# A hybrid attention layer: two query tiles of each band-attention head turned by VectorE and DMA instead of TensorE, and attention's outputs stored in one piece

## The chip, the cores and the metric

The kernel runs on one core of one Trainium2 chip. The metric is device time in microseconds (us) of one execution; less is better. Three runs of the kernel before gave 814.21, 815.94 and 815.33 us, with a median of 815.33.

The engines are TensorE (PE; its weight loads are shown as PEld), VectorE (DVE), ScalarE (ACT), GpSimd (POOL) and SyncE (SP), which issues all the DMAs of this kernel.

## What is computed

One layer on a prompt of 1024 frames and on a sample of 32 frames (with 512 cached keys and values), all in float32. Cut to what matters here:

```
[qA kA vA gA qB kB vB gB] = rmsnorm(h) @ w_in        # 1024 x 4096
A, 8 heads of 64: s = q k^T / 8 + bias[clip(k_pos - q_pos)]
                  a frame reads its own 64-frame chunk and the 8 chunks before it
                  w = softmax(s);  oA = w v
B, 8 heads of 64: z = q k^T / 8, strictly causal
                  w = sigmoid(z) * prod over later keys of sigmoid(-z);  oB = w v
y = concat(oA * silu(gA), oB * silu(gB)) @ w_out
h = h + rmsnorm(y)
h = h + sigmoid(h @ w_ple_gate) * (p @ w_ple)
```

The outputs are h of prompt and sample, and the new keys and values.

## The kernel before

**Numbers.** A float32 product is made of float32r products: each operand is split into a rounded part and a rest ("h" and "l" in the names), and two or three products are added in PSUM.

**Stages.** After a start that normalises x and turns it, the projection w_in is computed in columns of 128 outputs (`col_steps`, L715): one column is three chunks of 352 frames, each of 24 matmuls into a PSUM bank "mm" (two banks). Two heads of A or B are a pair; the eight pairs come in the order A0, B0, A1, B1, A2, B2, A3, B3 (L1160). While a pair's attention runs, the three columns k, q, v of the next pair are woven in (`weave`, L1228), and in the last stage the eight gate columns. Pairs with an odd number also carry the sample's attention for four heads (`sample_attention`, L926); the first four stages carry sums of w_out and w_ple_gate on POOL (`sum_weights`, L1264). At the end come the output projection and the gate, by a seven-product scheme.

**One head's attention** (`attention`, L781) has eight query tiles of 128. For A, tile i reads the key blocks max(0, i - 4) to i (`lo_block`), so tiles 4 to 7 have five blocks each. `scores(i)` (L798) makes the scores in PSUM banks "S", adds bias and takes the maximum on DVE into w0 (name "om"), takes the exponential on ACT into w1 ("be") and scales w1 on POOL. `weights_t(i)` (L845) turns w1, block by block: up to four PE transposes into a PSUM bank "T" (ptw), then ACT copies the rounded part to wTh and DVE takes the rest to wTl. `values(g)` (L882) multiplies four query tiles at once into the bank "PV" (PVA, PVB), and the result goes out in two halves of 256 columns: an ACT copy, a DVE add (the products of rounded and rest parts of v lie in different partitions) and a store to `o_dr`. Tiles are turned two units after their scores (LAG_T) and a group of four gets its values right behind its last tile's turn (LAG_V).

**Room.** w0 and w1 come from rings (`Arena`, L212) of 3076 and 3384 columns of 128 partitions, handed out in order from the front and again from the front when the end is reached; a new tile waits for the last use of all that it covers. wTh and wTl are rings of 33 blocks. The sample's cached keys and values lie in w1's ring, too. A head of A needs 30 blocks of 128 columns in each ring.

**Order.** Nothing is run in program order. A recorder (L268) takes down all operations, and `order` (L375) is a list planner: each engine has an estimated cost for each operation (`cost`, L342), PE takes attention (class 0) before columns (class 1) and then the lower program index, the other engines the lower index, and each takes the best of what is ready. A DMA holds SP for ISSUE ns, and its data count as there after DMA_NS, its size over DMA_RATE and DMA_MARGIN. The order found is fixed in the program: each engine runs its list strictly in that order, and an instruction that waits holds all behind it on its engine. All instructions are recorded at L453, so views by line show one line, and names tell them apart (the pair's number and the head are left out of the names: SA, ptwA, otB).

**Another place that turns by squares.** `values_out` (L681) turns v, 128 x 1024: DVE transposes 32 x 32 squares (vx), a store to a scratch in DRAM (swap), four loads that put the squares' rows in place, one for each quarter of the partitions, and an ACT copy that also restores the order of the blocks. `weights_t` holds the same path for a tile, behind `swapped`, which is always False.

Of the kernel before, what the change touches and what calls it, by code (L numbers as in the profile page):

```python
# [28 lines left out]

def swapped(ab, p, h, i):  # L30

    return False

LAG_T = 2
# [148 lines left out]
MARGIN = 400  # L185
ISSUE = 450
DMA_NS, DMA_RATE, DMA_MARGIN = 1500, 320.0, 2000
# [271 lines left out]
def stream_step(  # L459
# [321 lines left out]
    def attention(ab, p, h):  # L781
# [13 lines left out]
        def lo_block(i):  # L795
            return max(0, i - 4) if ab == "A" else 0

        def scores(i):  # L798
            L, kd, kl = Lq[h], KDh[h], KLD[h]
# [45 lines left out]
        def weights_t(i):  # L845
            g = i // 4
            step, size = LAID[ab, g]
            if g not in wT:
                wT[g] = [x.tile([P, size * P], f"{x.name}{nm}_{g}") for x in (ringh, ringl)]
            b0 = lo_block(i)  # L850
            w0, w1 = state.pop(i)
            n = i + 1 - b0
            at_ = ((i - 4 * g) * step + b0) * P
            hi, lo = (x[:, at_:at_ + n * P] for x in wT[g])
            if swapped(ab, p, h, i):

                nc.vector.transpose(w0[:, 0:n * P].rearrange("p (c b q) -> p b c q", c=4, q=32), w1)
                dr = scratch([P, n * P], f"swap{nm}_{i}")
                dma(dr, w0[:, 0:n * P])
                for c in range(4):  # L860
                    x = dr[:, c * n * 32:(c + 1) * n * 32].rearrange("(g k) x -> k g x", k=32)
                    dma(w1[32 * c:32 * c + 32].rearrange("k (g x) -> k g x", g=4), x)
                src = w1.rearrange("p (g b q) -> p g b q", g=4, q=32)
                hi, lo = (x.rearrange("p (b g q) -> p g b q", g=4, q=32) for x in (hi, lo))
                nc.scalar.copy(hi, src)
                nc.vector.tensor_tensor(lo, src, f(hi), ALU.subtract)
# [15 lines left out]
        def values(g):  # L882
# [20 lines left out]
        def cost(i):  # L903
            return i + 1 - lo_block(i)

# [20 lines left out]
    def sample_attention(ab, gi):  # L926
# [45 lines left out]
        def scores():  # L972
# [31 lines left out]
            dma(Vc, cv[0, 0, :, h4, :].rearrange("(b p) h d -> p b (h d)", p=P))  # L1004
            vn = at.tile([NS, 256], F32, tag="ot", name="vn" + nm, bufs=3)
            dma(vn, vs_dr[ab][:, 256 * gi:256 * gi + 256])
# [33 lines left out]
        def values():  # L1040
            acc = psum("PV", f"PV{nm}")[:, 0:256]
            for b, (w, v) in enumerate(bx["wv"]):
                for x, y in ((0, 0), (0, 1), (1, 0)):
                    nc.tensor.matmul(acc, w[x], v[y], start=(b + x + y == 0), stop=(b == 4 and x == 1))
            for h in range(4):
                src = acc[h * NS:(h + 1) * NS, h * HD:(h + 1) * HD]
                (nc.scalar.copy if h % 2 else nc.vector.tensor_copy)(diag[0:NS, h * HD:(h + 1) * HD], src)

        def out():
            pt = psum("T", f"pto{nm}")  # L1050
            for a in range(2):
                nc.tensor.transpose(pt[:, a * P:(a + 1) * P], diag[:, a * P:(a + 1) * P], ident)
            Os = at.tile([P, 2, NS], F32, tag="ot", name="O" + nm, bufs=3)
            nc.vector.tensor_copy(Os, pt[:, 0:2 * P].rearrange("p (a q) -> p a q", a=2)[:, :, 0:NS])
# [249 lines left out]

    ones = at.tile([P, P], F32R, tag="ot", name="ones", bufs=3)
    nc.gpsimd.memset(f(ones), 1.0)
# [520 lines left out]
```

## Time and profile before

| | |
|---|---|
| median of 3 runs | 815.33 us (814.21 to 815.94) |
| profiled execution | 815.1 us, its span 813.3 us |
| mean granted TensorE clock | 0.998 |
| DMA | 135.83 MB, 55.7% of 16 engines' span |
| DMAs issued by SP | 620 |

A row of a group of instructions reads: line, engine, operation, tile written <- tiles read, partitions x elements, count | busy us, mean ns of one | idle us of its engine just before them, and what ended that. A row of a tile's view gives the durations of its instructions as min/median/max in ns, and when the first and the last started. The chain of waits is followed back from the last instruction, at each step to what released it. A row of it, or of a timeline, gives start, length, engine, name and count.

### The profile page before, as it was taken

The numbers are of one execution on the slowest core, as the hardware profiler recorded it, in microseconds if no ns is written. First come the engines' busy times: TensorE is split into PE (matmuls) and PEld (weight loads), VectorE is DVE, ScalarE is ACT, GpSimd is POOL, SyncE is SP. The second block draws the span as 40 slices with busy tenths as digits, with TensorE's granted clock in tenths as the row PEclk, the third lists the DMA queues.
The fourth block names the chain that finished last, engine by engine and source line by source line (L and its number), as shares of the span: only waits on it lengthen the run. The fifth ranks groups of instructions, "written<-read, shape, count | busy, mean of one in ns | idle before, by whom it ended". The sixth has DMA issues, their size and how long they took to land.

```text
span 813.3 us, 14716 instructions
## 1 busy us (share of the span) xinstructions
PE 800.3 (98%) x4814; PEld 739.0 (91%) x4814; DVE 576.3 (71%) x1159; ACT 536.8 (66%) x1179; POOL 495.9 (61%) x551
## 2 busy tenths in 40 slices
PE   8999999999999999999999999999999999999997
PEld 6999999999999998999999999999998877888786
DVE  7627778687788798766778677873555677587655
ACT  5636886786486587775777587553447857876841
POOL 6625887985687678735553444775553537499513
PEclk9999999999999999999999999999999999999999
DMA  8419844546764645623413544343489947759744
GB/s 287 136 49 276 214 119 145 156 136 217 181 202 133 178 130 166 146 75 87 99 40 115 129 120 146 114 133 112 137 271 290 291 147 251 238 174 343 236 134 129
DMA packets 138430, 135.83 MB, mean 167 GB/s; under 512 B 36641, under 2 KB 104393, under 8 KB 138354
## 3 DMA queue, kind: packets, MB, share of 16 engines
q1 hardware_dynamic: 138354, 134.90, 55.7%
q8 instruction: 38, 0.62, 0.3%
q14 instruction: 38, 0.31, 0.1%
HBM read 85.54 MB, written 40.92 MB: 155 GB/s over the span
## 4 chain that ended last, share of the span: by engine, by line
PE 89%; ACT 4%; DMA 2%; POOL 2%; DVE 1%; issue 1%; SPq 0%; POOLq 0%
PE mm_gB L453 6%; PE mm_kB L453 6%; PE mm_qA L453 5%; PE mm_qB L453 5%; PE mm_kA L453 5%; PE mm_gA L453 5%; PE mm_vA L453 5%; PE PVB L453 4%; PE mm_vB L453 4%; PE SB L453 4%; PE ptwB L453 4%; PE SA L453 3%; PE PVA L453 3%; PE ptwA L453 3%; PE g0P L453 2%; PE g1P L453 2%
## 5 line engine op out<-in xcount | busy, mean ns | idle before, releaser
L453 POOL TENSOR_TENSOR be<-be,om 128x128 f32<-128x128 f32 (+8 forms) x66 | 90.5, 1379 | 67.9 <-DVE om L453 27.4
L453 DVE TENSOR_TENSOR_SCAN om<-om 128x512 f32<-128x512 f32 (+8 forms) x66 | 102.3, 1562 | 8.1 <-ACT om L453 7.8
L453 POOL TENSOR_SCALAR be<-be,statA 128x640 f32<-128x640 f32 (+2 forms) x64 | 42.6, 670 | 45.2 <-DVE statA L453 34.0
L453 ACT CAST wTh<-ptwB 128x512 fp32r<-128x512 f32 (+3 forms) x96 | 44.3, 483 | 25.3 <-PE ptwB L453 24.0
L453 DVE TENSOR_TENSOR wTl<-ptwB,wTh 128x512 fp32r<-128x512 f32 (+3 forms) x96 | 50.0, 545 | 14.0 <-ACT wTh L453 13.6
L453 DVE TENSOR_TENSOR wTl<-ptwA,wTh 128x512 fp32r<-128x512 f32 (+2 forms) x96 | 44.8, 482 | 16.4 <-ACT wTh L453 15.6
L453 ACT ACTIVATE om<-SB 128x384 f32<-128x384 f32 (+5 forms) x96 | 47.5, 499 | 11.7 <-DVE SB L453 9.2
L453 ACT ACTIVATE be<-om,statA 128x640 f32<-128x640 f32 (+2 forms) x64 | 44.7, 700 | 10.5 <-DVE statA L453 7.8
L453 ACT CAST wTh<-ptwA 128x512 fp32r<-128x512 f32 (+2 forms) x96 | 39.0, 426 | 15.7 <-PE ptwA L453 15.2
L453 ACT ACTIVATE be<-SB 128x384 f32<-128x384 f32 (+5 forms) x96 | 45.5, 506 | 4.5 <-DVE Vl2sB L453 1.5
L453 PE MATMUL ptwB<-ident,be 128*128 128x128 f32 x288 | 44.0, 273 | 0.7 <-DVE OsB L453 0.7
L453 PE MATMUL ptwA<-ident,be 128*128 128x128 f32 x240 | 39.2, 273 | 0.0
L453 PEld LDWEIGHTS ptwB<-ident,be 128*128 128x128 f32 x288 | 35.2, 140 | 3.2 <-DVE OsB L453 0.9
L453 PE MATMUL SB<-kdB,LB 128*128 128x384 f32 (+5 forms) x96 | 34.2, 361 | 0.8 <-ACT be L453 0.8
L453 PE MATMUL SB<-klB,LB 128*128 128x384 f32 (+5 forms) x96 | 33.9, 355 | 0.0
L453 POOL TENSOR_TENSOR oB<-oB,oB 128x256 f32<-128x256 f32 x32 | 31.5, 997 | 3.6 <-DMA oB<-in_w_out_dram 3.5
L453 DVE CUSTOM_DVE_ANT_0 om<-SA,biasA 128x320 f32<-128x320 f32 (+2 forms) x64 | 30.9, 482 | 3.9 <-PE SA L453 3.7
L453 PE MATMUL SA<-kdA,LA 128*128 128x320 f32 (+2 forms) x96 | 30.0, 320 | 1.1 <-DVE LA L453 1.1
L453 PEld LDWEIGHTS ptwA<-ident,be 128*128 128x128 f32 x240 | 29.8, 140 | 0.9
L453 POOL TENSOR_TENSOR gB<-gB,gB 128x256 f32<-128x256 f32 x32 | 29.4, 936 | 1.4 <-DMA gB<-in_w_ple_gate_dram 1.1
L453 PE MATMUL SA<-klA,LA 128*128 128x320 f32 (+2 forms) x96 | 29.6, 317 | 0.0
L453 POOL TENSOR_TENSOR h<-h,x 128x512 f32<-128x512 f32 (+1 forms) x18 | 23.0, 1297 | 0.8 <-DVE h L453 0.8
(711 smaller groups left out, 2652.5 us busy)
## 6 DMA issues: line engine op xcount, KB each, us to landing
oB<-in_w_out_dram SPq DMA_DIRECT2D x16, 256.0 KB, 3.5
sum_dro<-oB SPq DMA_DIRECT2D x16, 256.0 KB, 2.2
gB<-in_w_ple_gate_dram SPq DMA_DIRECT2D x16, 256.0 KB, 3.7
sum_drg<-gB SPq DMA_DIRECT2D x16, 256.0 KB, 2.4
x<-in_x_prompt_dram SPq DMA_DIRECT2D x16, 256.0 KB, 4.1
h_dr<-h SPq DMA_DIRECT2D x8, 512.0 KB, 3.6
ht<-h_dr SPq DMA_DIRECT2D x8, 512.0 KB, 5.7
raw<-sum_drg SPq DMA_DIRECT2D x16, 256.0 KB, 2.8
```

What stands on the lines that cost most here:

```text
L453: getattr(getattr(tc.nc, o.what[0]), o.what[1])(*args, **kw)
```

## The change

There are four edits.

1. Query tiles 4 and 6 of each A head are no longer turned by PE. ROUND names groups of tiles that share a room and one trip through DRAM; for A the groups are (4,) and (6,), one tile each, and B has none. DVE transposes w1 in squares into w0, w0 is stored to DRAM, four loads bring it back into w1, and one ACT copy and one DVE subtraction make wTh and wTl from w1, both for all five blocks.
2. `values` takes the result out in one piece of 512 columns for each group of four query tiles.
3. The tag "ot" has two buffers of 512 columns in place of three of 256. The sample's Qh and Ql share one. `diag`, which had a tile of its own set to nought once, comes from w1's ring and is set to nought for each of the four sample groups.
4. The planner's ISSUE is 600 ns, it was 450.

```diff
-def swapped(ab, p, h, i):
-    return False
+ROUND = {"A": ((4,),(6,)), "B": ()}
...
-ISSUE = 450
+ISSUE = 600
...
+        together = {i: g for g in ROUND[ab] for i in g}
+        whole, done_with = {}, []
+
+        def rooms(i):
+            more = ab == "B"
+            g = together.get(i, (i,))
+            if g not in whole:
+                n = sum(cost(x) for x in g) * P
+                whole[g] = ring0.tile([P, n + more * len(g)], f"om{nm}_{i}"), ring1.tile([P, n], f"be{nm}_{i}")
+            k, n = g.index(i), cost(i) * P
+            a = sum(cost(x) for x in g[:k]) * P
+            w0, w1 = whole[g]
+            return w0[:, a + more * k:a + more * k + n + more], w1[:, a:a + n]
...
-            w0 = ring0.tile([P, n + (ab == "B")], f"om{nm}_{i}")
-            w1 = ring1.tile([P, n], f"be{nm}_{i}")
+            w0, w1 = rooms(i)
...
-            if swapped(ab, p, h, i):
-                nc.vector.transpose(w0[:, 0:n * P].rearrange("p (c b q) -> p b c q", c=4, q=32), w1)
...
+            if i in together:
+                group = together[i]
+                done_with.append((i, hi, lo))
+                if i != group[-1]:
+                    return
+                w0, w1 = whole[group]
+                m = sum(cost(x) for x in group)
+                first = {x: sum(cost(y) for y in group[:k]) for k, x in enumerate(group)}
+                squares = w0[:, 0:m * P].rearrange("p (c b q) -> p b c q", c=4, q=32)
+                for x, _, _ in done_with:
+                    y = slice(first[x], first[x] + cost(x))
+                    nc.vector.transpose(squares[:, y], w1[:, y.start * P:y.stop * P])
+                dr = scratch([P, m * P], f"swap{nm}_{i}")
+                dma(dr, w0[:, 0:m * P])
                 for c in range(4):
+                    x = dr[:, c * m * 32:(c + 1) * m * 32].rearrange("(g k) x -> k g x", k=32)
                     dma(w1[32 * c:32 * c + 32].rearrange("k (g x) -> k g x", g=4), x)
+                turned = w1.rearrange("p (g b q) -> p g b q", g=4, q=32)
+                for x, hi, lo in done_with:
+                    src = turned[:, :, first[x]:first[x] + cost(x), :]
+                    hi, lo = (y.rearrange("p (b g q) -> p g b q", g=4, q=32) for y in (hi, lo))
+                    nc.scalar.copy(hi, src)
+                    nc.vector.tensor_tensor(lo, src, f(hi), ALU.subtract)
+                done_with.clear()
                 return
...
-            for x in range(2):
-                c = slice(2 * x * P, (2 * x + 2) * P)
-                ot = at.tile([P, 2 * P], F32, tag="ot", name=f"ot{nm}_{g}_{x}", bufs=3)
-                nc.scalar.copy(ot[r], acc[o, c])
-                nc.vector.tensor_tensor(ot[r], acc[r, c], ot[r], ALU.add)
-                dma(o_dr[sidx(ab, p)][r, (4 * g + 2 * x) * P:(4 * g + 2 * x + 2) * P], ot[r])
+            ot = at.tile([P, 4 * P], F32, tag="ot", name=f"ot{nm}_{g}", bufs=2)
+            nc.scalar.copy(ot[r], acc[o])
+            nc.vector.tensor_tensor(ot[r], acc[r], ot[r], ALU.add)
+            dma(o_dr[sidx(ab, p)][r, 4 * g * P:4 * (g + 1) * P], ot[r])
...
-    diag = at.tile([P, 256], F32, tag="diag", name="diag")
-    nc.gpsimd.memset(diag, 0.0)
...
-            Qf = at.tile([P, 2, P], F32, tag="ot", name="Qf" + nm, bufs=3)
-            Qh = at.tile([P, 2, P], F32R, tag="ot", name="Qh" + nm, bufs=3)
-            Ql = at.tile([P, 2, P], F32R, tag="ot", name="Ql" + nm, bufs=3)
+            Qf = at.tile([P, 2, P], F32, tag="ot", name="Qf" + nm, bufs=2)
+            Qh, Ql = (x[:, y] for x in [at.tile([P, 2, 2, P], F32R, tag="ot", name="Q" + nm, bufs=2)] for y in range(2))
...
+            diag = bx["diag"] = ring1.tile([P, 256], "diag" + nm)
+            nc.gpsimd.memset(diag, 0.0)
```

More of the change, by code (lines that the diff above doesn't have):

```diff
@@ L796, in lo_block, with cost @@
             return max(0, i - 4) if ab == "A" else 0
+        together = {i: g for g in ROUND[ab] for i in g}
+        whole, done_with = {}, []
+        def cost(i):
+            return i + 1 - lo_block(i)
+        def rooms(i):
[8 more added lines that the diff above has]
+            return w0[:, a + more * k:a + more * k + n + more], w1[:, a:a + n]
         def scores(i):
@@ L854, in weights_t @@
             hi, lo = (x[:, at_:at_ + n * P] for x in wT[g])
-            if swapped(ab, p, h, i):
-                nc.vector.transpose(w0[:, 0:n * P].rearrange("p (c b q) -> p b c q", c=4, q=32), w1)
-                dr = scratch([P, n * P], f"swap{nm}_{i}")
-                dma(dr, w0[:, 0:n * P])
+            if i in together:
[12 more added lines that the diff above has]
+                dma(dr, w0[:, 0:m * P])
                 for c in range(4):
-                    x = dr[:, c * n * 32:(c + 1) * n * 32].rearrange("(g k) x -> k g x", k=32)
+                    x = dr[:, c * m * 32:(c + 1) * m * 32].rearrange("(g k) x -> k g x", k=32)
                     dma(w1[32 * c:32 * c + 32].rearrange("k (g x) -> k g x", g=4), x)
[L863 to L866, printed above, removed]
+                turned = w1.rearrange("p (g b q) -> p g b q", g=4, q=32)
[5 more added lines that the diff above has]
+                done_with.clear()
                 return
@@ L895, in values @@
             o = slice((1 - h) * HD, (2 - h) * HD)
-            for x in range(2):
-                c = slice(2 * x * P, (2 * x + 2) * P)
-                ot = at.tile([P, 2 * P], F32, tag="ot", name=f"ot{nm}_{g}_{x}", bufs=3)
-                nc.scalar.copy(ot[r], acc[o, c])
-                nc.vector.tensor_tensor(ot[r], acc[r, c], ot[r], ALU.add)
-                dma(o_dr[sidx(ab, p)][r, (4 * g + 2 * x) * P:(4 * g + 2 * x + 2) * P], ot[r])
-        def cost(i):
-            return i + 1 - lo_block(i)
+            ot = at.tile([P, 4 * P], F32, tag="ot", name=f"ot{nm}_{g}", bufs=2)
+            nc.scalar.copy(ot[r], acc[o])
+            nc.vector.tensor_tensor(ot[r], acc[r], ot[r], ALU.add)
+            dma(o_dr[sidx(ab, p)][r, 4 * g * P:4 * (g + 1) * P], ot[r])
         out = {("B",): (0.0, begin)}
@@ L1004, in scores @@
             dma(Vc, cv[0, 0, :, h4, :].rearrange("(b p) h d -> p b (h d)", p=P))
-            vn = at.tile([NS, 256], F32, tag="ot", name="vn" + nm, bufs=3)
+            vn = at.tile([NS, 256], F32, tag="ot", name="vn" + nm, bufs=2)
             dma(vn, vs_dr[ab][:, 256 * gi:256 * gi + 256])
@@ L1050, in out @@
             pt = psum("T", f"pto{nm}")
+            diag = bx["diag"]
             for a in range(2):
                 nc.tensor.transpose(pt[:, a * P:(a + 1) * P], diag[:, a * P:(a + 1) * P], ident)
-            Os = at.tile([P, 2, NS], F32, tag="ot", name="O" + nm, bufs=3)
+            Os = at.tile([P, 2, NS], F32, tag="ot", name="O" + nm, bufs=2)
             nc.vector.tensor_copy(Os, pt[:, 0:2 * P].rearrange("p (a q) -> p a q", a=2)[:, :, 0:NS])
@@ L1301, in with_sample @@
         return out
-    ones = at.tile([P, P], F32R, tag="ot", name="ones", bufs=3)
+    ones = at.tile([P, P], F32R, tag="ot", name="ones", bufs=2)
     nc.gpsimd.memset(f(ones), 1.0)
```

## The prediction

> **What bounds the kernel now.** First the page: its first line, the engines' busy time, and the chain that ended last.
>
> ```profile
> span 813.3 us, 14716 instructions
> PE 800.3 (98%) x4814; PEld 739.0 (91%) x4814; DVE 576.3 (71%) x1159; ACT 536.8 (66%) x1179; POOL 495.9 (61%) x551
> ...
> PE 89%; ACT 4%; DMA 2%; POOL 2%; DVE 1%; issue 1%; SPq 0%; POOLq 0%
> ```
>
> The profiled run took 815.1 us for a span of 813.3, so 1.8 lie outside it; the median of the runs shown is 815.33, 0.2 more. PE is busy for all but 13.0 us of the span. A mean over the span can hide a stage with another limit, so next I read the busy times stage by stage. I cut where the attention of a pair gives way to the next: A0, B0, A1, B1, A2, B2, A3, B3, then the gates that are left.
>
> ```profile
> 67.00:124.00 57.00, 56.92 (x376) 55.41 (x375) 42.80 (x130) 45.16 (x106) 41.08 (x53) 1.00 0.70 200
> 124.00:190.00 66.00, 66.00 (x432) 63.94 (x430) 53.28 (x99) 47.40 (x106) 54.82 (x54) 1.00 0.53 160
> 190.00:250.00 60.00, 59.16 (x394) 57.09 (x394) 48.03 (x121) 40.97 (x97) 41.31 (x55) 1.00 0.65 183
> 250.00:320.00 70.00, 68.88 (x451) 65.74 (x450) 59.55 (x106) 49.60 (x114) 52.15 (x53) 1.00 0.55 156
> 320.00:372.00 52.00, 51.74 (x343) 50.30 (x342) 36.26 (x109) 38.48 (x93) 28.41 (x40) 1.00 0.44 107
> 372.00:440.00 68.00, 68.00 (x444) 65.82 (x443) 51.56 (x101) 48.96 (x110) 38.66 (x38) 1.00 0.35 92
> 440.00:498.00 58.00, 58.00 (x391) 56.55 (x390) 42.70 (x120) 39.87 (x94) 25.91 (x34) 1.00 0.44 117
> 498.00:584.00 86.00, 85.32 (x550) 82.42 (x549) 56.71 (x92) 45.95 (x106) 52.72 (x49) 1.00 0.45 131
> ```
>
> Columns: stretch and length, then busy us of PE, PEld, DVE, ACT and POOL, granted clock, DMA share, GB/s. PE's idle time is 0.08, 0, 0.84, 1.12, 0.26, 0, 0 and 0.68: 3.0 us in 517. So in attention the time is the sum of PE's work. Work taken from PE shortens the span, as long as some other work stands ready for it; that work is the projection columns woven in. Where does the cover get thin? At the end of B1.
>
> ```profile
> 300.00:312.00 12.00, 10.88 (x72) 10.21 (x71) 10.93 (x19) 10.64 (x22) 11.92 (x6) 1.00 0.43 125
> ```
>
> Here POOL is full, DVE and ACT nearly so, and PE stands for 1.1 us: the columns are used up and attention is late. This place I call the pinch.
>
> **The change part by part.** *Transposes off PE.* Of A's eight heads, tiles 4 and 6 have five key blocks each: 16 tiles, 80 of the 240 PE transposes. What is one worth? Two views give different answers: the group's mean, and the chain of waits in 290 to 320 us, where a run of them is followed start to start.
>
> ```profile
> L453 PE MATMUL ptwA<-ident,be 128*128 128x128 f32 x240 | 39.2, 273 | 0.0
> ...
> 291.53 0.55 PE ptwB L453 x5
> ...
> 313.89 0.87 PE ptwB L453 x8
> ```
>
> 273 ns is how long one is in the pipeline; five follow each other in 0.55 us and eight in 0.87, so each holds PE for 0.11. Same instruction, same shape in A and B. 80 x 0.11 = **8.8 us off PE**, 1.1 us per head, 2.2 per A stage. The Trainium skill ("TensorE: Matmul & The Clock Gate", Part 4: PE-mode transpose) gives about 275 ns for a PE transpose inside a kernel. The group row agrees with that as a duration, the chain rows do not as a pitch; taken as PE's time it would make the gain 22 us.
>
> *What takes their place.* Per tile: a VectorE transpose of 128x640 in 32x32 squares, a store of 320 KB, four loads of 80 KB, one ACT copy and one DVE subtraction of 128x640. The V path of before already works this way, on 128x1024; the keys' path has the transpose on 128x512.
>
> ```profile
> L453 DVE STREAM_TRANSPOSE ktA<-stkA x4: 692/702/712, 57.9 to 390.1; 128x512 f32<-128x512 f32 x4
> ...
> L453 DVE STREAM_TRANSPOSE vxB<-stvB x4: 1214/1245/1246, 127.8 to 490.8; 128x1024 f32<-128x1024 f32 x4
> L453 SPq DMA_DIRECT2D swapB<-vxB x4: 319/335/374, 129.0 to 492.1; - x4
> ...
> L453 SPq DMA_DIRECT2D stvB<-swapB x16: 374/428/2346, 133.9 to 500.2; - x16
> ...
> DMA to landing us min/median/max: 2.7/3.2/4.3
> ...
> L453 ACT COPY vtB<-stvB x4: 1047/1051/1054, 139.8 to 505.4; 128x1024 f32<-128x1024 f32 x4
> ...
> L453 DVE TENSOR_TENSOR v2B<-vtB,v2B x8: 661/693/2487, 141.5 to 507.7; 128x512 fp32r<-128x512 f32 x8
> L453 ACT CAST wTh<-ptwA x96: 248/420/605, 72.6 to 491.6; 128x128 fp32r<-128x128 f32 x40, 128x512 fp32r<-128x512 f32 x40, 128x256 fp32r<-128x256 f32 x8, 128x384 fp32r<-128x384 f32 x8
> L453 DVE TENSOR_TENSOR wTl<-ptwA,wTh x96: 252/481/693, 73.1 to 492.5; 128x128 fp32r<-128x128 f32 x40, 128x512 fp32r<-128x512 f32 x40, 128x256 fp32r<-128x256 f32 x8, 128x384 fp32r<-128x384 f32 x8
> ```
>
> The DVE transpose of 640, between 0.70 at 512 and 1.245 at 1024: 0.84 us (estimate). The subtraction, with both inputs in SBUF now: 0.69 at 512, so 0.86 for 640; before, the two pieces of 512 and 128 from PSUM took at most 0.69 + 0.25 = 0.94. ACT: 1.05 at 1024 gives 0.66 to 0.75 for 640, before 0.61 + 0.25 = 0.86. So DVE gets 0.84 - 0.08 = 0.76 more per tile, 3.0 per A stage, and ACT loses about 0.1 per tile. DVE's other end: that subtraction has once taken 2.49, which would be 1.8 more for each of 16. The Trainium skill ("SBUF — State Buffer", Who interferes with whom) has a reason: a DVE instruction with two SBUF inputs contends with a GpSimd instruction that reads SBUF. Here, the median of eight is at the low end, so I take that.
>
> *Latency.* In the first B column the transpose starts at 127.8 and ACT's copy at 139.8: 12.0 us; in the last 490.8 to 505.4: 14.6. The new path is smaller, but its hops are the same: 11 to 14 us from weights to transposed weights, where PE, ACT and DVE now need 2 to 3 (0.55 + 0.86 + 0.94). Behind each new wait stand: on SP the four loads and all later DMAs, on ACT the copy and all evacuations behind it, on DVE the subtraction. The planner counts a DMA with its margin, so it sets these where the data should have come. What waits for the tile is the second value product of the head, and the w1 and w0 room in the rings. PE has columns to run meanwhile, except at the pinch. SP issues 5 more per tile, at 0.34 to 0.43 us each: 80 more, about 33 us over 517.
>
> *Outputs in one piece.* Per group of four tiles two ACT copies, two DVE adds and two stores of 64 KB become one each.
>
> ```profile
> L453 DVE TENSOR_TENSOR otA<-PVA,otA 64x256 f32<-64x256 f32 x32 | 12.1, 417 | 12.3 <-ACT otA L453 12.3
> ...
> L453 ACT COPY otA<-PVA 64x256 f32<-64x256 f32 x32 | 10.2, 367 | 14.8 <-PE PVA L453 14.8
> ```
>
> One ACT copy of 512 columns costs 0.61 (wTh's largest form) for 2 x 0.37, one DVE add 0.69 for 2 x 0.42: 0.13 and 0.14 less, 32 times, 4 us off each engine. The bank is free after 0.61 + 0.69 = 1.30; in halves it was 0.37 + 0.42 + 0.42 = 1.21. Nothing on PE. SP issues 32 fewer. The rooms of Qf, Q, vn and O go from three to two but Q's halves share one, and diag's memsets, four on POOL, are hidden by PE's columns: nought.
>
> *The planner's ISSUE of 600.* It only re-orders. If the new order is better it can win at most PE's idle in the attention stages, 3.0 us; I put the same on the other side, as an estimate, and take nought.
>
> *What PE gives back.* By the pinch PE has saved two A stages, 4.4 us, and reaches the end of its columns that much sooner. Attention there is held by DVE, ACT and POOL, which the change doesn't relieve but loads. If A1 began sooner by as much, nothing is given back; if attention stays where it is, 4.4; if it comes later by the DVE work of A1 too (3.0 us, where DVE is already close to full), 7.4. Is it full there?
>
> ```profile
> 211.00:234.00 23.00, 22.66 (x154) 21.61 (x153) 18.99 (x62) 16.22 (x38) 13.84 (x23) 1.00 0.74 209
> ```
>
> DVE is busy for 19.0 of 23 us while A1 makes way for B1. I take **3.4 us**, near the middle between 0 and 7.4. Elsewhere there is cover: after B3 a run of gate matmuls stands alone.
>
> ```profile
> 583.72 32.66 PE mm_gB L453 x202
> ```
>
> So attention may end some 30 us later against PE's work without cost. Sum: 815.1 - 8.8 + 3.4 = 809.7, plus 0.2 to the median: **809.9 us**.
>
> **The rivals.** *All of it stays.* The column work starts each stage, so attention begins sooner and the pinch moves along: 815.3 - 8.8 = 806.5, with a better order down to 803.5. For it: PE's idle is nearly nought everywhere. Against it: 300 to 312.
>
> *It eats itself up.* The pinch gives back 7.4 and the order loses something too: 814 to 817, no change to speak of.
>
> *Slower: the ring of w1 holds the next head.* The ring has 3384 columns, and counting the tiles into it, tile 4 of a first head must be free before tiles 2 and 3 of the second can be written, five score tiles after it. How fast are scores made? SA's matmuls by windows:
>
> ```profile
> 60.00:75.00 15.00, 4.12 (x18) 1.00 0.90 276
> 75.00:90.00 15.00, 4.12 (x18) 1.00 0.89 217
> 90.00:105.00 15.00, 2.65 (x12) 1.00 0.78 216
> 105.00:120.00 15.00, 0.00 (x0) 1.00 0.46 130
> ```
>
> 48 matmuls are 16 tiles in some 31 us, 1.9 each; five tiles are 9.7 us. A hold of 12.0 to 14.6 is 2.3 to 4.9 too long, in each of 8 heads: 18 to 39 us of attention. The sample groups' tiles make the ring tighter in A1 and A3, and DMA is busy at 0.70 to 0.90 in A0, so landings can only get worse. It decides the sign from the point where PE has no columns left: it needs over 8.8 of the 18, half of it. Price if all of the lower end reaches PE: 815.3 - 8.8 + 18 = 825. Against it: in A0 no score is left after 105, while the chain of waits still has columns there at the end of the stage; this is the cover.
>
> ```profile
> 124.11 2.53 PE mm_vB L453 x16
> ```
>
> *A PE transpose is worth its 273 ns*: 80 x 0.273 = 21.8, 793.5 us. This is the Trainium skill's figure above; the chain rows speak plainly against it.
>
> That the change does not do what it says can be ruled out but for one thing: each group holds one tile, so no two tiles share a store.
>
> **How the numbers follow.** Forecast 809.9, own range 806.5 to 813.9 (nought to 7.4 given back): 0.52. All stays, 803.5 to 806.5: 0.18. Eats itself up, 814 to 817: 0.10. Slower by the ring, 817 to 827: 0.18. 273 ns: 0.02. A measurement of this kernel tells apart about 0.2%, 1.6 us: faster is below 813.7, same up to 817.0. Faster 0.52 + 0.18 + 0.02 = 0.72; same 0.10; slower 0.18. The range from 804.0 to 820.0 leaves out the 0.02, about 0.03 of the second case below it and 0.12 of the fourth above it.
>
> **What would show it.** Right: ptwA falls from 240 to 160 and PE's busy time to about 791.5; 16 new square transposes of 0.84 us; ot in 32 pieces fewer; PE idle of 2 to 5 us around the end of B1, waiting on ACT or DVE; no other stage with over 1 us of new idle. Wrong on size: PE busy falls by more or less than 8.8. Wrong on the pinch: its idle stays at 1.1 or exceeds 7. The ring would show as scores of a second head that wait on ACT or DVE for tiles 4 and 6, and PE idle in A stages. A stall of ACT's or DVE's queue on the swap's loads, over 1 us for most of the 16 tiles, would be a mechanism that I put at nought.

## The result and the profile after

The changed kernel takes 812.85 us (median of 20 runs, 810.95 to 816.87), the kernel before in the same session 814.84 (20 runs, 814.19 to 815.94). The ratio is 0.9975, 95% interval 0.9966 to 0.9983: faster by 2.0 us, where 5.4 were forecast. PE has been relieved as forecast; most of it came back, and not at the pinch.

The page of the changed kernel, its first line and the engines' busy time:

```profile
span 812.1 us, 14543 instructions
...
PE 795.2 (98%) x4734; PEld 733.6 (90%) x4734; DVE 594.7 (73%) x1127; ACT 536.2 (66%) x1133; POOL 499.8 (62%) x554
```

PE has 80 instructions fewer. At 0.11 us each that is 8.8 us of work, but its busy time fell by 5.1 and the span by 1.2 (813.3 to 812.1). So this execution gave back 8.8 - 1.2 = 7.6 us, some of it inside "busy". The groups that the change made, with count | busy, mean:

```profile
L449 PE MATMUL ptwA<-ident,be 128*128 128x128 f32 x160 | 26.7, 274 | 0.1
...
L449 DVE TENSOR_TENSOR wTl<-be,wTh 128x640 fp32r<-128x640 f32 x16 | 14.9, 929 | 4.8 <-ACT wTh L449 4.7
...
L449 DVE STREAM_TRANSPOSE om<-be 128x640 f32<-128x640 f32 x16 | 13.4, 837 | 1.2 <-POOL be L449 1.2
...
L449 ACT CAST wTh<-be 128x640 fp32r<-128x640 f32 x16 | 11.6, 728 | 1.7 <-DMA be<-swapA 1.7
...
L449 DVE TENSOR_TENSOR otA<-PVA,otA 64x512 f32<-64x512 f32 x16 | 11.0, 688 | 9.2 <-ACT otA L449 8.9 <-DMA be<-swapA 0.2
```

The sizes are those of the estimates (0.84, 0.86, 0.66 to 0.75 and 0.69 us); only the subtraction is 0.07 above, pulled up by single ones (one of 1.76 below). ACT stood 1.7 us in all for the trip's loads: the planner sets its copy late enough. The same stretches as before, and the pinch:

```profile
67.00:124.00 57.00, 56.52 (x366) 54.79 (x365) 45.14 (x127) 44.23 (x99) 38.78 (x49) 1.00 0.85 237
124.00:190.00 66.00, 66.00 (x430) 63.60 (x429) 56.46 (x97) 48.48 (x104) 53.66 (x52) 1.00 0.52 147
190.00:250.00 60.00, 56.21 (x353) 53.87 (x353) 45.72 (x110) 39.06 (x82) 38.23 (x51) 0.97 0.75 211
250.00:320.00 70.00, 67.26 (x436) 64.05 (x435) 61.91 (x91) 48.01 (x107) 51.32 (x55) 1.00 0.57 159
320.00:372.00 52.00, 52.00 (x339) 50.22 (x338) 44.01 (x122) 41.08 (x92) 39.93 (x49) 1.00 0.68 191
...
300.00:312.00 12.00, 12.00 (x81) 11.71 (x80) 11.25 (x15) 9.93 (x20) 10.47 (x6) 1.00 0.72 206
```

At the pinch, 300 to 312, PE is now busy for all 12.00 us (10.88 before). A wait of 0.87 us for DVE is left a little later:

```profile
316.71 0.95 PE L449 MATMUL ptwB<-ident,be 128*128 128x128 f32 x7 [0.87 <-DVE OsB L449]
```

The loss lies at 190 to 250, in A1: 56.21 us busy for 59.16, and a granted clock of 0.97, which is 0.03 x 60 = 1.8 us more. That is 4.8 us; B1, 250 to 320, adds 1.6. Together 6.4 of the 7.6. Of PE's 3.8 us of idle time in A1, 2.2 lie in the hole that is read next; the other 1.6 are waits for ACT at 235 to 243, where the kernel before has 0.5.

What stands behind the hole in A1 is seen in several views. First the chain of waits of the changed kernel:

```profile
212.31 0.48 PE mm_qB L449 x3
212.79 0.07 PE SA L449
212.87 7.29 DMA wr_vB<-in_w_in_dram
220.16 0.02 issue
220.18 0.63 ACT wh_vB L449
220.81 0.04 issue
220.85 3.30 PE mm_vB L449 x12
```

The weights of B1's value column were issued at 212.87, took 7.29 us to land, and ACT could round them only at 220.18. PE's timeline there, with its idle time and what ended it in brackets:

```profile
216.97 1.13 PE L449 MATMUL mm_qB<-hnl,wh_qB 128*128 128x352 f32 x6
220.05 0.41 PE L449 MATMUL SA<-kdA,LA 128*128 128x320 f32 x1 [1.95 <-DVE statA L449]
```

PE ends its column of B1's queries at 218.1 and stands for 1.95 us: no column can be had, and attention isn't ready either. The windows show the clock that followed (the column after POOL's):

```profile
215.00:220.00 5.00, 3.10 (x21) 2.80 (x19) 2.42 (x9) 1.08 (x3) 2.40 (x3) 1.00 1.05 321
220.00:225.00 5.00, 4.71 (x18) 4.35 (x19) 4.05 (x6) 4.43 (x9) 3.98 (x6) 0.66 0.60 218
```

Behind 1.95 us of idle time come 5 us at a granted clock of 0.66: 1.7 us more, booked as busy.

In the kernel before the weights were there long before PE needed them. SP's and ACT's timelines of before:

```profile
213.10 1.02 SPq L453 DMA_DIRECT2D wr_vB<-in_w_in_dram  x2
...
216.90 0.62 ACT L453 CAST wh_vB<-wr_vB 128x512 fp32r<-128x512 f32 x1 [1.11 <-DMA wr_vB<-in_w_in_dram]
```

They went out at the same time, 213.1, and landed sooner. And PE had more of the query column left. The matmuls of that column alone (72 in all) by windows; of before:

```profile
190.00:218.00 28.00, 11.12 (x60) 9.73 (x60) 0.93 (x2) 1.00 0.80 213
218.00:226.00 8.00, 2.66 (x13) 1.98 (x12) 0.32 (x1) 1.00 0.39 127
```

of after:

```profile
190.00:218.00 28.00, 13.57 (x72) 11.68 (x72) 0.93 (x2) 1.00 0.83 216
218.00:226.00 8.00, 0.10 (x1) 0.00 (x0) 0.46 (x1) 0.79 0.66 217
```

The column counts stand in brackets. Before, 60 matmuls were done by 218 and the rest covered PE until 225; after, all 72 were. PE has spent its cover early. Attention has less ready, too: the second value product (PVA) of A1's first head starts at 223.95 us, before at 216.66. It needs the tile whose trip these rows show; DVE, SP and ACT by their timelines:

```profile
194.72 0.84 DVE L449 STREAM_TRANSPOSE om<-be 128x640 f32<-128x640 f32 x1
...
213.93 0.90 SPq L449 DMA_DIRECT2D be<-swapA  x1
...
221.57 0.72 ACT L449 CAST wTh<-be 128x640 fp32r<-128x640 f32 x1
222.33 1.76 DVE L449 TENSOR_TENSOR wTl<-be,wTh 128x640 fp32r<-128x640 f32 x1 [0.92 <-ACT wTh L449]
```

From squares to the rest's end 29.4 us, for tile 6 of A1's first head: its last load is issued 19 us after its squares and lands 7.4 us later, and ACT's copy starts 27 us after the squares. Counted from the start of the squares to the end of the subtraction, the 16 trips took 12.9 to 29.4 us, ten of them over 16. The 11 to 14 us of the prediction ended with the start of ACT's copy; counted so, they took 10.8 to 26.9 us, nine of them under 14, and the longest are one in A0 (17.7) and two in A1 (18.8 and 26.9).

The late landing isn't the weights' alone. SP issued three loads within 1.6 us: the sample's cached values at 212.39, the weights at 212.87, the trip's last load at 213.93. They took 6.7, 7.3 and 7.4 us to land. DVE stood for the first of them, ACT for the second, each with all that comes after it in its list:

```profile
219.10 0.43 DVE L449 CAST Vh0sA<-be 128x512 fp32r<-128x512 f32 x1 [2.16 <-DMA be<-in_cache_a_v_dram]
...
220.18 0.62 ACT L449 CAST wh_vB<-wr_vB 128x512 fp32r<-128x512 f32 x1 [3.65 <-DMA wr_vB<-in_w_in_dram]
```

And the room in w1's ring is held. The scores of the second head's tiles 2 and 3 (384 and 512 columns) have left DVE by 212.8; their exponentials start at 224.12 and 224.84, the first of them released by the end of the trip's subtraction (222.33 + 1.76 = 224.09). Before, they started at 214.60 and 219.34.

```profile
224.12 0.72 ACT L449 ACTIVATE be<-om,statA 128x512 f32<-128x512 f32 x1 [0.39 <-DVE wTl L449]
```

### The profile page after: what moved, and what is told of

The parts are those of the page before. It is cut to its first block, busy times and chain, and to the rows that moved or that the text cites. A ratio compares the mean times of both kernels' runs of the same rounds, so it can differ in the third digit from the quotient of the medians.

```text
span 812.1 us, 14543 instructions
## 1 busy us (share of the span) xinstructions
PE 795.2 (98%) x4734; PEld 733.6 (90%) x4734; DVE 594.7 (73%) x1127; ACT 536.2 (66%) x1133; POOL 499.8 (62%) x554
## 4 chain that ended last, share of the span: by engine, by line
PE 88%; DMA 3%; POOL 3%; ACT 3%; DVE 2%; issue 1%; SPq 0%; ACTq 0%; POOLq 0%; DVEq 0%
PE mm_gB L449 6%; PE mm_gA L449 6%; PE mm_kB L449 5%; PE mm_vA L449 5%; PE mm_kA L449 5%; PE mm_qA L449 5%; PE mm_qB L449 5%; PE PVB L449 4%; PE SB L449 4%; PE mm_vB L449 4%; PE ptwB L449 4%; PE SA L449 3%; PE PVA L449 3%; PE g0P L449 2%; PE g1P L449 2%; PE o3P L449 2%
## 5 line engine op out<-in xcount | busy, mean ns | idle before, releaser
L449 POOL TENSOR_TENSOR be<-be,om 128x512 f32<-128x512 f32 (+8 forms) x66 | 92.9, 1417 | 64.0 <-DVE om L449 28.8
L449 DVE TENSOR_TENSOR_SCAN om<-om 128x256 f32<-128x256 f32 (+8 forms) x66 | 103.9, 1589 | 5.9 <-ACT om L449 5.1
L449 POOL TENSOR_SCALAR be<-be,statA 128x640 f32<-128x640 f32 (+3 forms) x64 | 47.2, 742 | 47.7 <-DVE statA L449 34.5
L449 ACT ACTIVATE be<-om,statA 128x640 f32<-128x640 f32 (+3 forms) x64 | 44.7, 698 | 14.0 <-DVE statA L449 10.3
L449 ACT CAST wTh<-ptwA 128x512 fp32r<-128x512 f32 (+2 forms) x64 | 25.8, 427 | 14.2 <-PE ptwA L449 13.5
L449 DVE TENSOR_TENSOR wTl<-ptwA,wTh 128x512 fp32r<-128x512 f32 (+2 forms) x64 | 29.6, 482 | 4.1 <-ACT wTh L449 3.4
L449 PE MATMUL SA<-klA,LA 128*128 128x320 f32 (+2 forms) x96 | 29.4, 314 | 0.0
L449 POOL TENSOR_TENSOR gB<-gB,gB 128x256 f32<-128x256 f32 x32 | 26.5, 852 | 0.6 <-DMA gB<-in_w_ple_gate_dram 0.3
L449 PE MATMUL ptwA<-ident,be 128*128 128x128 f32 x160 | 26.7, 274 | 0.1
L449 POOL TENSOR_TENSOR sggB<-sggB,oggB 128x352 f32<-128x352 f32 x12 | 14.2, 1186 | 14.5 <-DVE sggB L449 10.3
```

Source lines behind the costliest of these rows:

```text
L449: getattr(getattr(tc.nc, o.what[0]), o.what[1])(*args, **kw)
```

## The experiments

Each is an edit to the changed kernel, unless it says otherwise. "Lost" is what a kernel gives back: 0.11 us for each transpose off PE, less what the ratio leaves of 814.8 us.

**Is the trip what costs, or VectorE's work?** Three runs: without the trip and the squares, without the trip alone, and with a trip of few bytes.

```diff
 # e4_bare: both go, w1 is read as if turned
-                    nc.vector.transpose(squares[:, y], w1[:, y.start * P:y.stop * P])
...
-                dma(dr, w0[:, 0:m * P])
...
-                    dma(w1[32 * c:32 * c + 32].rearrange("k (g x) -> k g x", g=4), x)
 # e5_squares_no_dma: squares stay, store and loads go as in e4_bare, and the squares are read from w0
...
+                turned = w0[:, 0:m * P].rearrange("p (g b q) -> p g b q", g=4, q=32)
 # e10_small_trip
+                dma(dr, w0[:, 0:32])
...
+                    dma(w1[32 * c:32 * c + 32, 0:32], dr[32 * c:32 * c + 32, :])
```

> The change, but tiles 4 and 6 of A's heads are not turned at all: ACT and DVE take the rounded and the rest part straight from w1, so the second value products of A are of weights that were not turned. No square transpose, no store, no loads. Theory 1: the whole 8.8 us stays, 805.5 to 807.5 us, with PE's lost time at 13 to 14 us as before. Theory 2: the collisions stay, 810 to 813 us.

> The change with DVE's square transposes but without the store and the four loads: ACT and DVE read the squares from w0, so the blocks of the tile are in the wrong place. Theory 1a (DVE's added work gives the time back): near the change, 811 to 813 us. Theory 1b (the DMA trip does: busy DMA engines and the late loads of the column weights): near the bare kernel, 806 to 808 us. Theory 2: 810 to 813 us.

> The change with the trip through DRAM cut to 32 columns: the store is 16 KB and the four loads 4 KB, in place of 320 and 80; the waits, the SP issues and the hold of w0 and w1 stay. The second value products of A are of weights that are not put in place. If the bytes on the DMA engines give the 7 us back (theory 1b as bandwidth): 806 to 808 us, as without DMA. If the length of the trip does it, by holding the rings and queues: 811 to 814 us, as the change.

| | us | ratio, 95% | lost of 8.8 |
|---|---|---|---|
| changed kernel | 812.85 | 0.9975 (0.9966 to 0.9983) | 6.8 |
| e4_bare | 807.64 | 0.992 (0.9902 to 0.9938) | 2.3 |
| e5_squares_no_dma | 806.07 | 0.989 (0.9873 to 0.9907) | -0.2 |
| e10_small_trip | 813.03 | 0.9976 (0.9964 to 0.9989) | 6.8 |

VectorE's transposes and subtractions cost nothing: with them and no trip all 8.8 are kept. (e4_bare, with less work still, took 1.6 us more; the two intervals just overlap, and no run says why.) The trip costs about 7 us, and taking most of its bytes away gives none of them back: with a store of 16 KB and loads of 4 KB the time is the same. The trips are as long as before, 13.3 to 19.9 us from squares to the subtraction's end. The loss moves, though. In the profile of e10_small_trip, whose execution was its slowest (815.89 us), A1 keeps PE at 59.90 of 60 us, and the holes are in B1's and A2's stretches (the second and third row):

```profile
190.00:250.00 60.00, 59.90 (x396) 58.34 (x396) 48.31 (x114) 43.34 (x92) 42.99 (x57) 1.00 0.69 192
250.00:320.00 70.00, 66.91 (x432) 63.11 (x431) 61.00 (x107) 49.39 (x109) 52.34 (x55) 1.00 0.53 149
320.00:372.00 52.00, 49.80 (x322) 47.83 (x321) 42.48 (x99) 38.23 (x85) 36.84 (x46) 1.00 0.56 150
```

The weights of B1's value column went out at 213.8 here, later than in the changed kernel, and were there sooner; the time to landing of both loads, here and in the changed kernel:

```profile
DMA to landing us min/median/max: 3.0/3.2/3.5
...
DMA to landing us min/median/max: 7.3/7.4/7.6
```

So transfers in each other's way have a part in the hole of A1. As the sole cause of the loss they fall, and a place alone doesn't explain it either.

**Is A1 the place?** Turned tiles in all stages but A1, and in A1 alone:

```diff
-        together = {i: g for g in ROUND[ab] for i in g}
 # e6_not_A1
+        together = {i: g for g in ROUND[ab] for i in g} if p != 1 else {}
 # e20_only_A1
+        together = {i: g for g in ROUND[ab] for i in g} if p == 1 else {}
```

> The change with tiles turned by squares in A0, A2 and A3 alone, A1's by PE: 12 tiles, 6.6 us off PE. Theory 1b with A1 as its place (sample, sums and swap together fill the DMA engines): only the 2.2 us of A1 are missing from the saving and the loss of 5 us in A1 goes, so 815 - 6.6 + 0 to 2 = 808 to 811 us, better than the change. If the loss belongs to all stages alike: 813 to 814 us.

> The counterpart of the run in which A1 had no turned tile: here A1 alone has them, 4 tiles, 20 PE transposes off (2.2 us of PE work), outputs in one piece and ISSUE 600 as in the changed kernel. Against the 808.6 us with A1 left out. If A1 is the place of the loss, whatever comes before it: 815 to 819, the saving of 2.2 us more than given back. If the loss in A1 needs A0's saving ahead of it (columns further on, loads pulled together): 811 to 814.

e6_not_A1: 808.62 us, 0.9924 (0.9911 to 0.9936). It takes 6.6 us off PE and loses 0.4. It beats both kernels. e20_only_A1: 812.34 us, 0.9981 (0.9967 to 0.9995): 2.2 off, 0.7 lost. So A1 can carry the trip when A0 hasn't had it, and the kernel can carry the trip in A0, A2 and A3; A0 and A1 together lose more than either (no run has these two alone). The column of B1's queries in e6_not_A1:

```profile
190.00:218.00 28.00, 9.95 (x52) 8.53 (x52) 0.93 (x2) 1.00 0.71 188
218.00:226.00 8.00, 4.21 (x20) 3.26 (x20) 0.00 (x0) 1.00 0.44 123
```

20 of its matmuls are left at 218 and cover PE. That A1 by itself would be slower than before did not come true: by these two runs the loss needs what A0 has brought forward.

**ACT's tables.** In the changed kernel ACT loads its tables 10 times, in the kernel before 8 times: two of A1's exponentials stand behind B1's first sigmoids.

```profile
234.04 1.28 ACT L449 ACT_TABLE_LOAD   x1
...
236.46 1.28 ACT L449 ACT_TABLE_LOAD   x1
237.76 0.83 ACT L449 ACTIVATE be<-om,statA 128x640 f32<-128x640 f32 x1
...
241.08 1.28 ACT L449 ACT_TABLE_LOAD   x1
```

The first row is due anyway; the others are 2.6 us more, where PE waits for ACT, 1.6 us in all. The Trainium skill ("ScalarE: Activation LUTs", What ACT_TABLE_LOAD costs) treats the load as an instruction of ACT's own, and the trace agrees: 1.28 us each, in line with the rest. Four runs bear on it. The first has no turned tiles at all: outputs in one piece, rooms and ISSUE 600 alone. The second adds a rule for the order, by which a B score's sigmoids come behind the last exponential on record. The third and fourth put the rule into the changed kernel, first as it is, then with the last sixteen exponentials.

```diff
 # e3_no_turn
-ROUND = {"A": ((4,),(6,)), "B": ()}
+ROUND = {"A": (), "B": ()}
 # e12_no_turn_tables (on e3_no_turn), e11_tables: behind each sigmoid of B's scores
+                    rec.ops[-1].after.add(EXPS[-1])
...
 # e18_tables
+                    rec.ops[-1].after.update(EXPS[-16:])
...
```

> The change without its turned tiles: outputs in one piece, the rooms, ISSUE of 600; PE turns all tiles. Theory 1 (PE's saving of 8.8 us is real and the load put on DVE, ACT and DMA gives 7 back): nothing of either is here, so 814 to 816 us, as before. Theory 2 (the new order as such, with its ISSUE of 600, runs into collisions, whatever is turned): the loss is here without the saving, 818 to 822 us.

> The kernel with outputs in one piece and ISSUE 600, no tile turned by squares, with the same rule for the tables. It took 819.6 us with 10 loads, two of them at 357 to 361 us, where PE waited 2.1 us for ACT. Table theory: 8 loads and 814 to 817 us. If the outputs in one piece or their two rooms cost by themselves: 818 to 820 us still.

> The change with one more rule for the planner: a B tile's sigmoids come behind the last exponential of A that was recorded before them, so that ACT changes its table once from A to B (the change loads a table 10 times, the kernel before 8 times). Table theory: 8 loads, the 1.6 us of idle at 235 to 243 us goes, 809 to 811.5 us. Theory 1b alone: the tables cost nothing, 812 to 814 us.

> The changed kernel with one rule more for the order: a B score's sigmoids come after the last sixteen exponentials on record, so no B1 sigmoid stands between two of A1's exponentials. The rooms stay as they are, the load of the cached values goes out late as in the changed kernel. 8 loads of ACT's tables in place of 10. If the two additional table loads and what stands behind them are the larger part of the 7.6 us: 807 to 809. If the late load of the cached values is the larger part (1.95 us of idle PE at 220 us and the lower granted clock after it): 810 to 812.

e3_no_turn: 819.63 us, 1.006 (1.0039 to 1.0081), slower by 4.9 with the same work. It loads the tables 10 times, two of them at a spot where PE waits for the sigmoid behind them:

```profile
357.49 1.28 ACT L449 ACT_TABLE_LOAD   x1
...
360.05 1.28 ACT L449 ACT_TABLE_LOAD   x1
361.34 0.55 ACT L449 ACTIVATE be<-SB 128x128 f32<-128x128 f32 x2
```

e12_no_turn_tables: 8 loads, 815.8 us, 1.0019 (1.0006 to 1.0032). There the rule for the tables is worth 3.8 us. In the changed kernel it isn't: e11_tables still has 10 loads (the last exponential on record isn't the last in ACT's order) and takes 812.03 us, 0.9975 (0.9962 to 0.9989); e18_tables has 8 and takes 816.79, 1.0031 (1.0011 to 1.0051), above both times that were expected. Its profile has less idle PE in A1 (57.51 us busy of 60, from 56.21) and as much in B1. And e9_halves and e7_sums_later, further down, have 12 loads and take 813.06 and 813.04 us. So the additional loads are no cause that stands by itself.

**Room or queue?** The sample's cached values lie in w1's ring, which the trip holds; their load goes out at 212.4 us in the changed kernel, 200.8 before. And SP issues nearly without a gap from 195.6 to 214, each issue 0.3 to 1.5 us. One run takes the values out of the ring; one takes the columns' weights off SP, one the trip's loads (in both the planner counts 450 ns of ACT for each issue).

```diff
 # e17_V_in_w0s_ring
-            Vc = ring1.tile([P, 4, 256], "Vc" + nm)
+            Vc = ring0.tile([P, 4, 256], "Vc" + nm)
 # e32_weights_by_ACT
+            (dma if j < 3 else nc.scalar.dma_start)(raw, w_in[0, kh * 512:(kh + 1) * 512, c0:c0 + P].rearrange("(k p) c -> p k c", p=P))
...
 # e32b_trip_by_ACT
+                    nc.scalar.dma_start(w1[32 * c:32 * c + 32].rearrange("k (g x) -> k g x", g=4), x)
...
```

> One edit to the changed kernel: the sample group's cached values take room in w0's ring in place of w1's, so that their load no longer queues for room that the turned tiles hold. All else stays: 16 turned tiles, 160 PE transposes, the trip through DRAM. Theory (what PE gives back comes from the room in w1's ring that the trip holds in A1, through the late load of the cached values and the exponentials that are put behind it): the load goes out near 200 us in place of 212, 8 loads of ACT's tables in place of 10, 807 to 809 us. Rival (what is given back comes from ACT's, DVE's and SP's queues standing behind the trip's loads, wherever the room is): 811 to 814. Second rival (w0's ring is the tighter one, om holding its squares until the store is done): 814 to 818.

> The changed kernel, its columns' input weights (from the fourth column on) loaded through ACT's DMA queue in place of SP's; the planner counts 450 ns of ACT for each issue and keeps 600 for SP's. The trip, its bytes, the rooms and the 160 PE transposes stay; ACT's tables are loaded 8 times in this order. In the changed kernel SP issues without a gap from 195.6 to 214 us, and the weights of B1's value column go out at 212.9 (213.1 in the kernel before) though PE stands there some 4 us sooner. Theory (what PE gives back comes of SP's queue, which the trip's loads fill, so that weights go out no sooner than before): weights out by 210 us, no idle of 1 us or more at 220, 806 to 809 us. Rival (the trip's length and the bytes in the way of the weights' landing, whatever the queue): 811 to 813. Worse than that, 814 to 818, if ACT's own issues cost it as much.

> The changed kernel with the trip's four loads per tile issued through ACT's DMA queue in place of SP's (64 loads off SP, its store stays there), 450 ns of ACT counted for each by the planner. 8 loads of ACT's tables in this order. Theory of SP's queue: the weights of B1's value column go out by 210 us in place of 212.9, 806 to 810 us. Rival (trip's length and bytes): 811 to 813. If 64 issues, each waiting for the store to land, hold up ACT's evacuations: 815 to 820.

e17_V_in_w0s_ring: 822.0 us, 1.0087 (1.0074 to 1.01). The load goes out at 197.8 and the tables are loaded 8 times, as the theory of the ring wanted, and it is the slowest of all. The cover is spent there as in the changed kernel (72 of the query column's matmuls by 218), and the weights go out later still, at 214.0:

```profile
214.01 5.79 DMA wr_vB<-in_w_in_dram
219.83 0.63 ACT wh_vB L449
220.50 1.71 PE mm_vB L449 x8
```

e32_weights_by_ACT: 816.71 us, 1.0012 (0.9995 to 1.0029); its weights go out at 213.8, no sooner. e32b_trip_by_ACT: 815.8 us, 1.0007 (0.999 to 1.0023); its weights go out at 211.2 and there is no hole at 220, but PE waits at other places, 2.0 us at 238 us for the rest of a tile's weights and 2.8 us in all for B's sigmoids. The Trainium skill ("DMA: Bandwidth & Descriptors", Rules for kernel authors) says that spreading DMAs over several engines' queues saves issue time only. Neither run gained anything (816.71 and 815.8 us), which agrees. By e32b_trip_by_ACT, SP's queue falls as the sole cause. w1's ring is not settled: e17_V_in_w0s_ring moved the cached values alone, the trip's tiles hold their rooms as before, and there the second head's tile 1 stands for the subtraction of A1's first trip:

```profile
208.56 0.51 ACT L449 ACTIVATE be<-om,statA 128x256 f32<-128x256 f32 x1 [1.84 <-DVE wTl L449]
```

No run took that hold away and kept the trip.

**The planner's ISSUE, and the outputs.**

```diff
 # e1_issue450
-ISSUE = 600
+ISSUE = 450
 # e2_before_issue600 (on the kernel before)
-ISSUE = 450
+ISSUE = 600
 # e9_halves: outputs in halves, three rooms and diag's own tile, as before
+            for x in range(2):
+                c = slice(2 * x * P, (2 * x + 2) * P)
...
```

> The change with the planner's ISSUE back at 450. Theory 1 (load on DMA and DVE): another order of the same work under the same load, 812 to 814 us. Theory 2 (collisions of one particular order): the time moves by 2 us or more either way, out of 811 to 815 us.

> The kernel before with ISSUE 600, nothing else. Theory 1: 814 to 816 us, PE's lost time at 12 to 15 us. Theory 2: the order alone costs, 817 us or more; or it wins up to 3 us, the idle time of PE in the attention stages.

> The change without the outputs in one piece: halves, three rooms of 256 columns, diag in its own tile; tiles 4 and 6 turned by squares, ISSUE of 600. If the outputs in one piece cost by themselves (the kernel with them and without turned tiles took 819.6): 807 to 810 us. If that was an unlucky order, any time from 808 to 818, told by the number of activation table loads on ACT: 8 with a time under 811, 10 or more with a time over it.

e1_issue450: 817.8 us, 1.0036 (1.0023 to 1.0049): with 450 the changed kernel is 5 us slower than with 600. e2_before_issue600: 815.1 us, 1.0008 (0.9997 to 1.0019): on the kernel before it makes no difference. Yet its profile has a hole at the same place, with no tile turned by squares: 57.56 us of PE in A1, a granted clock of 0.66 in 220 to 225, and a wait of 2.44 us:

```profile
221.42 1.34 PE L453 MATMUL PVA<-wTh,v2A 128*128 128x512 f32 x4 [2.44 <-ACT wTh L453]
```

That execution took 815.95 us: a hole there isn't the trip's mark alone, and doesn't settle the time. e9_halves: 813.06 us, 0.9993 (0.9979 to 1.0007): with the outputs in halves the turned tiles gain 0.6 instead of 2.0, and the two intervals overlap; the one piece does no harm and may be worth a us or two. There, too, all 72 matmuls of the query column are done by 218, but the weights are rounded from 216.87 on, and PE is busy 5.00 and 4.83 us in the two windows of 215 to 225. So the spent cover alone makes no hole; the late weights belong to it.

**Is the crowd in A1 and B1 what counts?** The sums of w_out and w_ple_gate load DMA, SP and POOL in the first four stages. Three runs move those of A1 and B1 to A2 and B2: in the changed kernel, in the kernel before and in e6_not_A1.

```diff
-        if n < 4:
-            att = with_sums(att, [("og"[n // 2], 2 * (n % 2) + i) for i in range(2)])
+        if n in (0, 1, 4, 5):
+            att = with_sums(att, [("og"[n // 4], 2 * (n % 2) + i) for i in range(2)])
```

> The change with the weight sums of A1 and B1 (16 loads and 16 stores of 256 KB, and their subtractions on POOL) put into A2 and B2, where the DMA engines were busy for less than half of the time before. Theory 1b (DMA engines full in A1): the column weights land in time, the idle and the lost clock in A1 go, and POOL's lock on DVE's copies in B1 with them: 807 to 810 us. Theory 1a (DVE's work): 812 to 813 us.

> Control: the kernel before with the same sums put later. Its lost time around A1 and B1 is 4 us, so at most 3 us can be won: 812 to 815 us by both theories.

> Turned tiles everywhere but in A1 (808.6 us when run alone) with the weights' sums of A1 and B1 moved to A2 and B2, which took the kernel before from 814.8 to 812.0. If the two gains come from different places they add up: 805 to 806.5. If both come from the same crowded stretch at the end of A1 and in B1: 808 to 809.

e7_sums_later: 813.04 us, 0.9989 (0.9972 to 1.0005), far from the 807 to 810 of full DMA engines; its A1 still has PE at 56.96 us, with B1 at 69.45. e8_before_sums_later: 812.02 us, 0.9967 (0.9955 to 0.9979), faster than the kernel before by 2.7 us with no other change. e14_not_A1_sums_later: 810.61 us, 0.9939 (0.9917 to 0.9961); three of its six times lie at 807.7 to 808.6 and three at 812.6 to 812.7, and the profiled one, of the upper three, has an idle stretch of 2.5 us on PE near 740 us, far behind the change. The two gains don't add up. e8_before_sums_later confirms that B1's stretch is crowded in the kernel before (70.00 us of PE in it, from 68.88), and no more.

## Why the prediction was right and wrong

**Right.** The range (812.85 in 804.0 to 820.0). The sign, with some luck: with ISSUE at 450 the same change is slower than the kernel before (e1_issue450). The pitch of 0.11 us: e5_squares_no_dma and e6_not_A1 gain 9.0 and 6.2 us where it says 8.8 and 6.6; at 273 ns it would have been over 20. PE's busy time, forecast at 791.5 us, is 791.8 in e5_squares_no_dma; in the changed kernel it is 795.2, with the stretch at the lower clock in it. The sizes of the new pieces. The stall of ACT's or DVE's queue on the loads at nought: 1.7 us on ACT in all. ISSUE at nought holds for the kernel before alone; with the turned tiles it moved the time by 5 us, outside of the 3.0 either way.

**Wrong: the term "What PE gives back".** It was put at 3.4 us and measured 7.6 in the profile (6.8 by the medians). Size, place and reason failed. The place was the pinch at the end of B1, since DVE, ACT and POOL are full there. But 300 to 312 us now has no idle PE at all, with 0.87 us left at 316. The reason was DVE's load, and e5_squares_no_dma shows that it costs nothing: what gives the time back is the trip through DRAM. The loss lies in A1 (4.8 us) and B1 (1.6), and the sign that was named for it, no other stage with over 1 us of new idle, is what the profile refutes.

**The step below it: "PE has columns to run meanwhile".** The 11 to 14 us of "Latency" held for nine of the sixteen tiles; the three longest trips, 17.7 to 26.9 us by the same ends, lie in A0 and A1, since squares, store, loads, copy and subtraction each stand in an engine's list behind other work. But cover was counted as if it cost nothing. It is true at that moment, and it is a loan: PE runs columns while attention waits, so the columns end sooner. In A1 the next column's weights have then not landed, and PE stands, then runs 5 us at a clock of 0.66. The query column's 72 of 72 matmuls by 218 us, against 60 before and 52 to 64 in e4_bare, e5_squares_no_dma, e6_not_A1 and e20_only_A1, fit this for A1; that the weights must be late as well is seen in e9_halves. No run tried it by itself.

**The rival of w1's ring** named a hold of the room as the mechanism, with PE's columns as the cover that decides. It priced the kernel at 817 to 827 us, which was too dear. Its sign is there all the same: PE idle in A1, and exponentials of a second head that stand for a trip's subtraction, in the changed kernel and in e17_V_in_w0s_ring. How much of the 7 us the hold is worth no run shows.

**What is shown and what stays open.** Shown: the trip through DRAM costs about 7 us, and VectorE's work none of it. By e6_not_A1 and e20_only_A1 it needs A1's trips and those of another stage; as the holes lie in A1 and B1, that is A0. Ten orders of the kernel with the full set of trips (the changed kernel, e1, e7, e9, e10, e11, e17, e18, e32, e32b) lie between 812.0 and 822.0 us; the four without the trip, or without it in A1, at 806.1 to 810.6. Open: by which of its steps the trip makes attention late. Small transfers, the rule for the tables, another room for the cached values and ACT's queue each changed where PE stands, and none gave time back. The order found by the planner also moves by some 5 us for the same work (e3_no_turn and e12_no_turn_tables, e1_issue450), so 2 us between two of these kernels says little of a mechanism. The lost clock in A1 is read from one profile of the changed kernel; it wasn't tried by itself. e11_tables has a hole of 1.24 us there, no lower clock after it, and takes 812.03 us.

## What to carry to other kernels

Work that fills an engine's waiting time is spent by it: where a change makes one chain later and another shorter, count how much of the filler is left at each later point and whether what it needs (here the next column's weights) comes sooner too. Price a new hop through DMA by the slowest trip of such kind in a full stage, not by the nearest quiet one, and try it stage by stage: leaving it out of one of four stages gave 808.6 us in place of 812.85.

## What the runs showed of the hardware

- 1.95 us without a matmul were followed by 5 us at a mean granted clock of 0.66, and 2.44 us in e2_before_issue600 as well; in e17_V_in_w0s_ring two such holes (2.63 and 2.83 us) brought the stretch of 190 to 250 us to 0.94. Not every hole did: after 1.99 us in e32b_trip_by_ACT, before 238.33, the clock stayed at 1.00.
- DVE's copies of 64x32 in SBUF can be far longer than their size: four of them in the changed kernel's B1 took 5.48 us while POOL was at work, and PE waited 1.08 us for what follows. The same copies for A took 0.15 to 0.45 us each.

```profile
272.30 5.48 DVE L449 COPY QfsB<-qsS 64x32 f32<-64x32 f32 x4
```

- One issue on SP took between 0.3 and 2.4 us in the changed kernel, and the same 256 KB of weights for B1's value column landed in 3.0 to 7.6 us: 3.8 to 5.0 in the kernel before, 7.3 to 7.6 in the changed one, 3.0 to 3.5 with the small trip.
